# Two-block transformer kernel on one core: the second RG-LRU gate product emitted between the first SSD blocks, SSD's decayed rows taken straight from the transposed rows, dt rows on VectorE

## The chip, the cores and the metric

The kernel runs on one core of one Trainium2 chip. The metric is device time in microseconds, from the start of the one launch to its end. Six names for the units of the core are used below: PE (TensorE, the matmul engine; PEld is its weight load), DVE (VectorE), ACT (ScalarE), POOL (GpSimd), SP (SyncE, which here only issues DMAs) and the DMA engines. Each engine works through its own instruction list in the order written in the program, and waits where an operand is not there yet; so an instruction that waits holds up everything behind it on its engine.

## The reference, cut to what matters

Two transformer blocks on one sequence of 1024 rows of width 1024, in float32. The change lies in the mixer of the second block. Its input projection feeds three mixers side by side, whose outputs are joined and multiplied by `w_out`:

```
z, xbc, dt_raw, u_s5, x_rg, g_rg = split(h @ w_in)
# SSD: chunks of 128 rows, 8 heads of 64 channels, state of 128
xbc = silu(causal_dwconv(xbc));  xs, bm, cm = split(xbc)
dt  = softplus(dt_raw + dt_bias);  adt = -exp(a_log) * dt;  a_cs = cumsum(adt in the chunk)
xdt = xs * dt
y_diag = (cm bm^T * exp(a_cs_l - a_cs_s), lower triangle) xdt
states = bm^T (exp(a_cs_last - a_cs) * xdt)          # the decayed rows
state  = state * exp(a_cs_last) + states             # carried from chunk to chunk
y = (y_diag + exp(a_cs) * (cm state_before) + xs * d_skip) * silu(z);  y = rms_norm(y) * w
# RG-LRU: width 256
y_rg = linear_scan(a, b) * gelu(g_rg)
# then
y = concat(y_ssd, y_s5, y_rg) @ w_out;  h = layer_norm(ALPHA * h + y);  cross attention;  MLP
```

## The kernel before

Float32 products are made of three matmuls of reduced-precision halves: every operand is split into a high part (a cast on ACT, line 82) and a low part (a subtraction on DVE, line 83), and `mm3` issues high x high, high x low, low x high (lines 114, 115, 116). A tile of 128 rows by 1024 columns so costs one cast and one subtraction before PE can use it.

`build` is a list of stages written as generators. A scheduler orders the instructions of each engine ahead of the run, following the order in which the generators emit them and the times that it expects; the order is fixed once the kernel is built. Buffers come from pools with a fixed number of tiles for each tag (`BUFS`): a tile of tag S is reused after six others of that tag, so the emission order also decides which load waits for which reader.

The stages around the change, in the order of emission:

- `dt_proj` (line 1170) makes dt, adt and, in `s_exp`, three sets of exponentials; set 1 is the decay to the chunk's end.
- `xbc_proj` makes the eight feature tiles of xbc (matmuls, a convolution of three DVE operations at line 1216, a tanh on ACT at 1237, a product on DVE at 1238) and stores each to DRAM (`s_xbc`, line 1239). It is interleaved with `s5_mixer` and `rg_mixer`.
- `rg_mixer` ends with the gate: for each of the two halves (m = 0, 1) 48 matmuls, two ACT evictions for each 512 columns (1393, 1394), gelu (DVE 1325, 1326, ACT 1327, DVE 1328), the product with the scan (1396) and a store (`rg_od`, 1397). Both halves are emitted in one step.
- `wout_load` loads `w_out` as eight tiles of 128x1024 (512 KB each, line 668), splitting each.
- `ssd_block(i)`, i = 0 to 7, in three steps run as a pipeline by `pipe` (block i's first step is emitted ahead of block i-1's second). Step 1: load of the block from `s_xbc` (1254) and of z (1256), PE transposes (1260, 1264), products of the B and C rows (1266), ACT copies (1261, 1268), the masked C-B tile (DVE 1270), xdt and the decayed rows (both on POOL, 1274 and 1275), the decay matrix (ACT 446, PE 1283, ACT 1284) and its mask product for two groups of heads (DVE 1285). Step 2: PE 1291 (state), 1295 (states), 1298 (diagonal), the new state (DVE 1300, 1301), y (DVE 1303, 1304, 1306, 1307; the d_skip product on POOL at 1305). Step 3: square sum (ACT 1310), a reciprocal root as a chain of small DVE operations (135 to 141), scaling (DVE 1313), transposes (PE 1316), ACT 446, store to `s_od` (1319).
- `block2_out` is woven in behind: for each of 8 row tiles it loads the three mixers' outputs (686), splits them (82, 83), runs 48 matmuls against the `w_out` tiles, adds the residual (DVE 1067, with statistics at 155), normalises (165 to 170 on DVE, 171 on ACT) and transposes (PE 182, ACT 186).

The first row tile of `block2_out` can start its matmuls when SSD block 0 is through all three steps and the `w_out` tiles are split.

Of the kernel before, what the change touches and what calls it, by code (L numbers as in the profile page):

```python
# [10 lines left out]
ALU = mybir.AluOpType  # L11
# [6 lines left out]
NB = 8  # L18
# [1083 lines left out]
class Mix2(Mix1):  # L1102
# [67 lines left out]
    def dt_proj(self, T):  # L1170
        nc, I = self.nc, self.I
# [13 lines left out]
        dt = self.small([128, 64], tag="s_dt", bufs=1)  # L1185
# [12 lines left out]
            nc.tensor.matmul(out=ps[:, 64 * k:64 * k + 64], lhsT=l, rhs=adt, start=True, stop=True)  # L1198
        self.s_exp = self.small([128, 3, 64], tag="s_exp", bufs=1)
        nc.scalar.activation(out=self.s_exp.rearrange("p a b -> p (a b)"), in_=ps[:, 0:192], func=ACTF.Exp)  # L1200

    def z_tile(self, T, t):
        nc = self.nc
# [43 lines left out]
    def ssd_block(self, i):  # L1247
        nc = self.nc
        sl = slice(128 * i, 128 * i + 128)
        hs = slice(8 * i, 8 * i + 8)  # L1250
        bc64 = lambda a: a.unsqueeze(2).broadcast_to([128, 8, 64])
        v64 = lambda a: a.rearrange("p (h c) -> p h c", c=64)
# [4 lines left out]
        xt = self.page("H")  # L1257
# [7 lines left out]
        for g in range(2):  # L1265
# [5 lines left out]
                                in1=self.tri[:, 0].unsqueeze(1).broadcast_to([128, 2, 128]))  # L1271
        xx = self.page("S")
        xdt, xdec = v64(xx[:, 0:512]), v64(xx[:, 512:1024])
        nc.gpsimd.tensor_tensor(out=xdt, in0=v64(xt[:, 0:512]), in1=bc64(self.s_dt[:, hs]), op=ALU.mult)
        nc.gpsimd.tensor_tensor(out=xdec, in0=xdt, in1=bc64(self.s_exp[:, 1, hs]), op=ALU.mult)
        sg = self.ps("sc")
        Ts = []
        for g in range(2):
# [51 lines left out]
    def rg_mixer(self, T):  # L1330
        nc, I = self.nc, self.I
# [56 lines left out]
        for m, (xc, r, gx, t) in enumerate(ms):  # L1388
            x, q = self.page("X"), self.page("X")
            for h in range(2):  # L1390
                sl = slice(512 * h, 512 * h + 512)
                ps = self.feat_out(T, Wg, slice(128 * m, 128 * m + 128), h)
                nc.scalar.activation(out=x[:, sl], in_=ps, func=ACTF.Copy, scale=0.5)
                nc.scalar.activation(out=q[:, sl], in_=ps, func=ACTF.Square)
            self.gelu(x, q, q)
            nc.vector.tensor_tensor(out=t, in0=t, in1=q, op=ALU.mult)
            nc.sync.dma_start(out=self.rg_od[:, m, :], in_=t)

    def cmul(self, ore, oim, a, b, t, eng=None):

# [428 lines left out]
def build(tc, I, out):  # L1829
    from contextlib import ExitStack  # L1830
    with ExitStack() as ctx:
        n = Mix2(tc, ctx, I, out)
        n.modulation()
        n.kv_mem()
        def run(g):
            while True:
                try:
                    next(g)
                except StopIteration as e:
                    return e.value  # L1840

        def delay(g, k):
            for _ in range(k):
                yield
            yield from g

        norm, kv = n.first_norm(I["x"]), n.kv_proj()
        T, steps = None, [3, 0, 1, 0, 1]
        while T is None:
# [4 lines left out]
            T = next(norm)  # L1854
# [13 lines left out]
        T = run(n.block1_out())  # L1868
        T = n.block1_mlp(T)
        n.dt_proj(T)  # L1870
        xbc = n.xbc_proj(T)
        for g, side in ((n.s5_mixer(T), (3, 1)), (n.rg_mixer(T), (1, 3))):
            for _ in g:
                for _ in range(side[0] if side else 0):
                    next(xbc, None)
                side = side[1:]
        run(xbc)
        n.ssd_setup()
        n.wout = n.wout_load(I["w_out_2"])
        out = n.block2_out()  # L1880
        T = next(out)
        run(n.weave(n.pipe(n.ssd_block(i) for i in range(NB)), delay(out, 3)))
        T = run(n.attention(T))
        n.block2_mlp(T)

# [85 lines left out]
```

## Time and profile before

| | |
|---|---|
| time before, median of 3 runs | 2657.97 us (2657.94 to 2659.93) |
| the profiled execution's own time | 2657.86 us |
| its span in the trace | 2655.9 us |
| PE busy | 2541.6 us, 96% of the span |
| DVE busy | 1879.1 us, 71% |
| ACT busy | 1172.0 us, 44% |
| POOL busy | 239.3 us, 9% |
| mean granted PE clock | 0.979 of full speed |

PE is busy for 96% of the span, so time is lost or won only where PE stands still or runs at the lower clock. The shares are averages over stages with different limits: in the first SSD blocks, at about 1590 to 1635 us, DVE is nearly full and PE waits.

### The profile page before, as it was taken

The numbers are of one execution on the slowest core, as the hardware profiler recorded it, in microseconds if no ns is written. First come the engines' busy times: TensorE is split into PE (matmuls) and PEld (weight loads), VectorE is DVE, ScalarE is ACT, GpSimd is POOL, SyncE is SP. The second block draws the span as 40 slices with busy tenths as digits, with TensorE's granted clock in tenths as the row PEclk, the third lists the DMA queues.
The fourth block names the chain that finished last, engine by engine and source line by source line (L and its number), as shares of the span: only waits on it lengthen the run. The fifth ranks groups of instructions, "written<-read, shape, count | busy, mean of one in ns | idle before, by whom it ended". The sixth has DMA issues, their size and how long they took to land. (4 is left out here: it accounts for less than half of the span.)

```text
span 2655.9 us, 33016 instructions
## 1 busy us (share of the span) xinstructions
PE 2541.6 (96%) x12086; PEld 2065.0 (78%) x12086; DVE 1879.1 (71%) x3205; ACT 1172.0 (44%) x1866; POOL 239.3 (9%) x222
## 2 busy tenths in 40 slices
PE   7899999889999999999999998999998999999997
PEld 6586777677888888888877776778876888888886
DVE  4858666678897777646865567785568777767786
ACT  3622233344654444433643474552237454444342
POOL 4121135540000000000000003100000000000000
PEclk8899999999999999999999999999998999999999
DMA  9772433464266569866632243361102755799783
GB/s 334 253 256 100 146 100 99 140 168 149 78 230 222 195 231 328 305 192 229 199 149 64 82 143 115 116 222 56 40 32 88 256 191 210 245 341 337 263 284 106
DMA packets 255130, 484.36 MB, mean 182 GB/s; under 512 B 21604, under 2 KB 110964, under 8 KB 254968
## 3 DMA queue, kind: packets, MB, share of 16 engines
q1 hardware_dynamic: 247768, 470.59, 52.2%
q10 hardware_dynamic: 7200, 11.67, 1.2%
q8 instruction: 95, 1.56, 0.3%
q14 instruction: 67, 0.55, 0.1%
HBM read 338.80 MB, written 143.38 MB: 182 GB/s over the span
## 5 line engine op out<-in xcount | busy, mean ns | idle before, releaser
L114 PE MATMUL ps<-U,W 128*128 128x512 f32 (+1 forms) x1080 | 427.3, 396 | 10.4 <-ACT ev L776 5.1
L115 PE MATMUL ps<-U,W 128*128 128x512 f32 (+1 forms) x1080 | 425.6, 394 | 1.5 <-DVE U L341 1.5
L114 PE MATMUL ps<-W,H 128*128 128x512 f32 x1088 | 424.4, 390 | 0.4 <-DVE X L1069 0.3
L116 PE MATMUL ps<-U,W 128*128 128x512 f32 (+1 forms) x1080 | 423.5, 392 | 0.8 <-DVE W L83 0.8
L83 DVE TENSOR_TENSOR W<-S,W 128x1024 fp32r<-128x1024 f32 (+1 forms) x272 | 333.1, 1228 | 128.5 <-ACT W L82 127.5
L115 PE MATMUL ps<-W,H 128*128 128x512 f32 x1088 | 423.9, 390 | 0.0
L116 PE MATMUL ps<-W,H 128*128 128x512 f32 x1088 | 423.9, 390 | 0.0
L82 ACT CAST W<-S 128x1024 fp32r<-128x1024 f32 x288 | 298.6, 1043 | 242.2 <-PE ps L115 161.1
L82 ACT CAST H<-S 128x1024 fp32r<-128x1024 f32 x130 | 136.6, 1050 | 287.4 <-PE ps L115 200.7
L83 DVE TENSOR_TENSOR H<-S,H 128x1024 fp32r<-128x1024 f32 x130 | 158.6, 1220 | 146.0 <-ACT H L82 141.2
L114 PEld LDWEIGHTS ps<-U,W 128*128 128x128 f32 (+1 forms) x1080 | 201.2, 186 | 60.9 <-ACT ev L776 5.4
L115 PEld LDWEIGHTS ps<-U,W 128*128 128x128 f32 (+1 forms) x1080 | 201.2, 186 | 49.5 <-DVE U L341 4.6
L114 PEld LDWEIGHTS ps<-W,H 128*128 128x128 f32 x1088 | 204.3, 188 | 43.4 <-DVE X L1069 1.2
L116 PEld LDWEIGHTS ps<-U,W 128*128 128x128 f32 (+1 forms) x1080 | 201.2, 186 | 46.8 <-DVE W L83 1.9
L116 PEld LDWEIGHTS ps<-W,H 128*128 128x128 f32 x1088 | 204.3, 188 | 41.9
L115 PEld LDWEIGHTS ps<-W,H 128*128 128x128 f32 x1088 | 204.3, 188 | 41.7
L116 PE MATMUL ps<-W,U 128*128 128x512 f32 x352 | 139.8, 397 | 5.5 <-DVE U L83 5.5
L114 PE MATMUL ps<-W,U 128*128 128x512 f32 x352 | 141.8, 403 | 2.6 <-DVE X L274 2.0
L115 PE MATMUL ps<-W,U 128*128 128x512 f32 x352 | 140.3, 398 | 0.0
L776 ACT ACTIVATE ev<-ev 128x512 f32<-128x512 f32 x104 | 65.5, 630 | 152.4 <-DVE ev L874 122.5
L116 PEld LDWEIGHTS ps<-W,U 128*128 128x128 f32 x352 | 67.0, 190 | 20.7 <-DVE U L83 6.8
L777 ACT ACTIVATE X<-ev 128x512 f32<-128x512 f32 x128 | 81.0, 634 | 3.5
(529 smaller groups left out, 4505.1 us busy)
## 6 DMA issues: line engine op xcount, KB each, us to landing
S<-mlp_h SPq DMA_DIRECT2D x112, 512.0 KB, 5.1
S<-in_w_ff SPq DMA_DIRECT2D x96, 512.0 KB, 5.1
mlp_h<-X SPq DMA_DIRECT2D x96, 512.0 KB, 4.2
S<-in_mlp_w SPq DMA_DIRECT2D x96, 512.0 KB, 4.9
mlp_w<-S SPq DMA_DIRECT2D x96, 256.0 KB, 2.5
S<-mlp_w SPq DMA_DIRECT2D x48, 512.0 KB, 4.8
S<-in_w_in SPq DMA_DIRECT2D x46, 512.0 KB, 5.3
X<-in_w_ada SPq DMA_DIRECT2D x32, 512.0 KB, 6.8
```

What stands on the lines that cost most here:

```text
L82: self.nc.scalar.copy(out=hi, in_=src)
L83: (lo_eng or self.nc.vector).tensor_tensor(out=lo, in0=src, in1=hi.bitcast(F32), op=ALU.subtract)
L114: mm(out=ps, lhsT=lh, rhs=rh, start=start and k == 0, stop=False)
L115: mm(out=ps, lhsT=lh, rhs=rl, start=False, stop=False)
L116: mm(out=ps, lhsT=ll, rhs=rh, start=False, stop=stop and k == n - 1)
L776: nc.scalar.activation(out=r, in_=x, func=ACTF.Relu)
L777: nc.scalar.activation(out=out, in_=r, func=ACTF.Square)
```

## The change

Four edits. In `dt_proj` the decay exponentials of all blocks are multiplied by dt once, in place (one new 128x64 product on DVE). In `ssd_block` the decayed rows are then made from the transposed rows and this product, no longer from xdt; xdt itself moves from POOL to DVE. `rg_mixer` yields after each half of the gate. `build` runs the first gate half, then emits the first step of SSD block 0, then the second gate half, then the first step of block 1 and the second of block 0, and only then `wout_load`; the weave with `block2_out` starts after two steps less, which leaves it where it was in terms of SSD steps.

```diff
--- before.py
+++ after.py
@@ -1198,6 +1198,7 @@
             nc.tensor.matmul(out=ps[:, 64 * k:64 * k + 64], lhsT=l, rhs=adt, start=True, stop=True)
         self.s_exp = self.small([128, 3, 64], tag="s_exp", bufs=1)
         nc.scalar.activation(out=self.s_exp.rearrange("p a b -> p (a b)"), in_=ps[:, 0:192], func=ACTF.Exp)
+        nc.vector.tensor_tensor(out=self.s_exp[:, 1], in0=self.s_exp[:, 1], in1=dt, op=ALU.mult)
 
     def z_tile(self, T, t):
         nc = self.nc
@@ -1271,8 +1272,8 @@
                                 in1=self.tri[:, 0].unsqueeze(1).broadcast_to([128, 2, 128]))
         xx = self.page("S")
         xdt, xdec = v64(xx[:, 0:512]), v64(xx[:, 512:1024])
-        nc.gpsimd.tensor_tensor(out=xdt, in0=v64(xt[:, 0:512]), in1=bc64(self.s_dt[:, hs]), op=ALU.mult)
-        nc.gpsimd.tensor_tensor(out=xdec, in0=xdt, in1=bc64(self.s_exp[:, 1, hs]), op=ALU.mult)
+        nc.vector.tensor_tensor(out=xdt, in0=v64(xt[:, 0:512]), in1=bc64(self.s_dt[:, hs]), op=ALU.mult)
+        nc.gpsimd.tensor_tensor(out=xdec, in0=v64(xt[:, 0:512]), in1=bc64(self.s_exp[:, 1, hs]), op=ALU.mult)
         sg = self.ps("sc")
         Ts = []
         for g in range(2):
@@ -1395,6 +1396,7 @@
             self.gelu(x, q, q)
             nc.vector.tensor_tensor(out=t, in0=t, in1=q, op=ALU.mult)
             nc.sync.dma_start(out=self.rg_od[:, m, :], in_=t)
+            yield
 
     def cmul(self, ore, oim, a, b, t, eng=None):
 
@@ -1869,17 +1871,25 @@
         T = n.block1_mlp(T)
         n.dt_proj(T)
         xbc = n.xbc_proj(T)
-        for g, side in ((n.s5_mixer(T), (3, 1)), (n.rg_mixer(T), (1, 3))):
-            for _ in g:
-                for _ in range(side[0] if side else 0):
-                    next(xbc, None)
-                side = side[1:]
+        side = [3, 1]
+        for _ in n.s5_mixer(T):
+            for _ in range(side.pop(0) if side else 0):
+                next(xbc, None)
+        rg = n.rg_mixer(T)
+        for k in (1, 3, 0, 0):
+            next(rg)
+            for _ in range(k):
+                next(xbc, None)
         run(xbc)
         n.ssd_setup()
+        ssd = n.pipe(n.ssd_block(i) for i in range(NB))
+        next(ssd)
+        run(rg)
+        next(ssd)
         n.wout = n.wout_load(I["w_out_2"])
         out = n.block2_out()
         T = next(out)
-        run(n.weave(n.pipe(n.ssd_block(i) for i in range(NB)), delay(out, 3)))
+        run(n.weave(ssd, delay(out, 1)))
         T = run(n.attention(T))
         n.block2_mlp(T)
```

How this moves the instructions. Two lines are inserted ahead of `build`: the lines named above as 1201 to 1397 are one higher in the changed kernel (1260 is 1261 there, 1285 is 1286), those behind 1397 two higher.

The list of PE before, at the end of the second gate half (`ps_12863` is its last product) and the start of SSD block 0 (`H_12952`):

```order
L114 MATMUL ps_12863<-U_6173,W_12521 128x512
L115 MATMUL ps_12863<-U_6174,W_12521 128x512
L116 MATMUL ps_12863<-U_6173,W_12522 128x512
L1260 MATMUL ps_12957<-ident,H_12952 128x128 x4
L1264 MATMUL ps_12963<-ident,H_12952 128x128 x2
L1266 MATMUL ps_12963<-H_12952 128x128 x2
L1283 MATMUL ps_12973<-half_12982,tri 128x512
L1283 MATMUL ps_13011<-half_13020,tri 128x512
L1291 MATMUL ps_13028<-half_12896,H_12952 128x256 x2
L1283 MATMUL ps_13070<-half_13071,tri 128x512
L1260 MATMUL ps_12995<-ident,H_12990 128x128 x4
```

And now, where the first product of the second gate half (`ps_12878`) is under way; `H_12838` is SSD block 0:

```order
L116 MATMUL ps_12878<-U_6171,W_12517 128x512
L114 MATMUL ps_12878<-U_6171,W_12516 128x512
L115 MATMUL ps_12878<-U_6172,W_12516 128x512
L1261 MATMUL ps_12843<-ident,H_12838 128x128 x4
L1265 MATMUL ps_12849<-ident,H_12838 128x128 x2
L1267 MATMUL ps_12849<-H_12838 128x128 x2
L116 MATMUL ps_12878<-U_6171,W_12517 128x512
L114 MATMUL ps_12878<-U_6171,W_12522 128x512
L115 MATMUL ps_12878<-U_6172,W_12522 128x512
L116 MATMUL ps_12878<-U_6171,W_12523 128x512
L114 MATMUL ps_12878<-U_6171,W_12522 128x512
```

Block 0's transposes stood behind the whole second gate half; they now stand after 11 of its 48 matmuls, and the other 37 stand behind them.

The list of DVE before, from the first gate half's last product (1396) on; the rows of line 83 split `w_out` tiles:

```order
L1396 TENSOR_TENSOR H_12528<-H_12528,X_12773 128x1024
L83 TENSOR_TENSOR X_12913<-S_12911,X_12912 128x1024
L83 TENSOR_TENSOR X_12919<-S_12917,X_12918 128x1024
L83 TENSOR_TENSOR W_12925<-S_12923,W_12924 128x1024
L83 TENSOR_TENSOR X_12937<-S_12935,X_12936 128x1024
L83 TENSOR_TENSOR W_12931<-S_12929,W_12930 128x1024
L1325 TENSOR_SCALAR X_12835<-X_12835 128x1024
L1270 TENSOR_TENSOR H_12956<-ps_12963,tri 128x256
L1326 TENSOR_TENSOR X_12835<-X_12835,X_12834 128x1024
L1285 TENSOR_TENSOR half_12974<-half_12974,H_12956 128x512
```

And now, from the second gate half's gelu (1327) on; `H_12942` is SSD block 1, line 1275 is xdt, the last row splits the first `w_out` tile:

```order
L1326 TENSOR_SCALAR X_12877<-X_12877 128x1024
L1275 TENSOR_TENSOR S_12956<-H_12942,s_dt_11569 128x512
L1327 TENSOR_TENSOR X_12877<-X_12877,X_12876 128x1024
L1271 TENSOR_TENSOR H_12942<-ps_12949,tri 128x256
L1301 TENSOR_TENSOR half_12835<-half_12835,s_exp_11603 128x512
L1286 TENSOR_TENSOR half_12960<-half_12960,H_12942 128x512
L1329 SCALAR_TENSOR_TENSOR X_12877<-X_12877,X_12876 128x1024
L1286 TENSOR_TENSOR half_12968<-half_12968,H_12942 128x512
L1397 TENSOR_TENSOR H_12546<-H_12546,X_12877 128x1024
L1302 TENSOR_TENSOR half_12835<-ps_12979,half_12835 128x512
L1304 TENSOR_TENSOR H_12838<-ps_12976,s_exp_11603 128x512
L83 TENSOR_TENSOR W_12999<-S_12997,W_12998 128x1024
```

The `w_out` splits, of which seven stood ahead of block 0's C-B tile and one behind the gate, now all stand behind the gate and block 0's state update, the first at the place shown and the other seven among blocks 0, 1 and 2.

The list of DVE before in the stretch in which row tile 2 of `block2_out` is split (`U_13216`) beside SSD block 5 (`half_13478`, `half_13486`) and step 2 of block 4 (`H_13273`):

```order
L1285 TENSOR_TENSOR half_13486<-half_13486,H_13460 128x512
L1301 TENSOR_TENSOR half_12896<-ps_13497,half_12896 128x512
L1303 TENSOR_TENSOR H_13273<-ps_13494,s_exp_11603 128x512
L170 TENSOR_SCALAR sm_13542<-sm_13540,sm_13544 128x1
L1304 TENSOR_TENSOR H_13273<-ps_13494,H_13273 128x512
L83 TENSOR_TENSOR U_13216<-S_13579,U_13215 128x8x128
L1306 TENSOR_TENSOR H_13273<-H_13273,H_13277 128x512
L1307 TENSOR_TENSOR H_13273<-H_13273,ev_13275 128x512
```

And the same stretch now, up to the split (`U_13217`):

```order
L1286 TENSOR_TENSOR half_13487<-half_13487,H_13461 128x512
L1302 TENSOR_TENSOR half_12835<-ps_13498,half_12835 128x512
L1304 TENSOR_TENSOR H_13274<-ps_13495,s_exp_11603 128x512
L139 TENSOR_SCALAR rs_13546<-rs_13546 128x1
L1305 TENSOR_TENSOR H_13274<-ps_13495,H_13274 128x512
L140 TENSOR_SCALAR rs_13546<-rs_13546 128x1
L1307 TENSOR_TENSOR H_13274<-H_13274,H_13278 128x512
L141 TENSOR_SCALAR sm_13545<-rs_13546,sm_13545 128x1
L1308 TENSOR_TENSOR H_13274<-H_13274,ev_13276 128x512
L170 TENSOR_SCALAR sm_13543<-sm_13541,sm_13545 128x1
L83 TENSOR_TENSOR U_13217<-S_13580,U_13216 128x8x128
```

Two products of block 4's y (1306 and 1307, here 1307 and 1308) stood behind the split and now stand ahead of it, and so does, some rows further up, block 5's xdt (1275 here). Of the same kind is a shift at row tile 0: block 4's C-B tile, its two mask products and block 3's state sum, which stood ahead of row tile 0's residual sums, now stand between those sums and the statistics' end (165).

## Rows read from the trace of the kernel before

**Rows 1.** Stretches: busy time of PE, PEld, DVE, ACT, POOL, then clock, DMA.

```profile
1571.40:1590.40 19.00, 18.69 (x82) 14.69 (x81) 14.97 (x14) 10.99 (x16) 0.00 (x0) 1.00 0.82 271
1590.40:1634.60 44.20, 33.95 (x176) 24.72 (x174) 40.37 (x69) 23.84 (x58) 18.08 (x13) 0.92 0.36 109
```

**Rows 2.** PE timeline: start, duration, line, tiles, idle before it and releaser.

```profile
1589.69 0.39 PE L114 MATMUL ps<-U,W 128*128 128x512 f32 x1
...
1590.15 0.39 PE L116 MATMUL ps<-U,W 128*128 128x512 f32 x1
...
1604.24 1.11 PE L1260 MATMUL ps<-ident,H 128*128 128x128 f32 x4 [0.38 <-DVE H L1270]
...
1633.30 1.10 PE L1295 MATMUL ps<-S,H 128*128 128x256 f32 x4 [0.23 <-ACT H L1261]
1634.24 0.60 PE L1316 MATMUL ps<-ident,H 128*128 128x128 f32 x4
...
1637.13 0.50 PE L116 MATMUL ps<-W,U 128*128 128x512 f32 x1 [1.37 <-DVE U L83]
...
1669.69 0.50 PE L116 MATMUL ps<-W,U 128*128 128x512 f32 x1 [2.21 <-DVE U L83]
...
1690.70 0.50 PE L116 MATMUL ps<-W,U 128*128 128x512 f32 x1 [1.94 <-DVE U L83]
...
1712.36 0.47 PE L116 MATMUL ps<-W,H 128*128 128x512 f32 x1
```

**Rows 3.** DVE timeline from the convolution's end to the first row tile.

```profile
1573.71 3.91 DVE L1216 SCALAR_TENSOR_TENSOR bc<-S,hw,bc 128x1023 f32<-128x1023 f32 x3
1578.81 1.23 DVE L1238 SCALAR_TENSOR_TENSOR bc<-S,bc 128x1024 f32<-128x1024 f32 x1 [1.19 <-ACT S L1237]
...
1583.44 1.22 DVE L1328 SCALAR_TENSOR_TENSOR X<-X,X 128x1024 f32<-128x1024 f32 x1 [1.19 <-ACT X L1327]
...
1593.81 1.73 DVE L1326 TENSOR_TENSOR X<-X,X 128x1024 f32<-128x1024 f32 x1
1595.46 2.97 DVE L1285 TENSOR_TENSOR half<-half,H 128x512 f32<-128x512 f32 x2
...
1635.02 2.06 DVE L83 TENSOR_TENSOR U<-S,U 128x1024 fp32r<-128x1024 f32 x1
```

**Rows 4.** POOL by line, 1571 to 1830 us: count, busy, mean ns, idle before.

```profile
L1305 POOL TENSOR_TENSOR H<-H,srow 128x512 f32<-128x512 f32 x8 | 12.1, 1510 | 0.0
L1275 POOL TENSOR_TENSOR S<-S,s_exp 128x512 f32<-128x512 f32 x8 | 10.4, 1306 | 0.6
L1274 POOL TENSOR_TENSOR S<-H,s_dt 128x512 f32<-128x512 f32 x8 | 9.9, 1233 | 253.4 <-ACT H L1261 253.4
```

**Rows 5.** SP timeline (the last xbc store, the first block's load).

```profile
1580.06 0.34 SPq L1239 DMA_DIRECT2D s_xbc<-bc  x1
...
1583.37 0.56 SPq L1254 DMA_DIRECT2D H<-s_xbc  x1
```

**Rows 6.** Line 1254, the loads of SSD blocks: time from issue to landing.

```profile
DMA to landing us min/median/max: 4.0/4.7/7.5
```

**Rows 7.** Line 668, the `w_out` loads: time from issue to landing.

```profile
DMA to landing us min/median/max: 3.3/4.7/8.1
```

**Rows 8.** DVE timeline beside row tiles 2 and 4.

```profile
1662.58 1.33 DVE L1285 TENSOR_TENSOR half<-half,H 128x512 f32<-128x512 f32 x1
1663.84 1.53 DVE L1300 TENSOR_TENSOR half<-half,s_exp 128x512 f32<-128x512 f32 x1
...
1668.42 1.22 DVE L83 TENSOR_TENSOR U<-S,U 128x1024 fp32r<-128x1024 f32 x1
1669.56 0.68 DVE L1306 TENSOR_TENSOR H<-H,H 128x512 f32<-128x512 f32 x1
1670.27 0.69 DVE L1307 TENSOR_TENSOR H<-H,ev 128x512 f32<-128x512 f32 x1
...
1710.45 1.22 DVE L83 TENSOR_TENSOR H<-S,H 128x1024 fp32r<-128x1024 f32 x1
```

## Prediction, made before the changed kernel was run

> **What bounds the kernel now.** I read the page's shares first, then the stretches around the change, then in them the PE and DVE timelines, and POOL and SP where they feed these. PE is the bound of the whole, so I ask where PE stands still. From 1571 to 1590 us it runs the gate products and hardly waits (18.69 busy of 19.00); from 1590.4 to 1634.6, the first SSD blocks, it is busy for 33.95 of 44.20 us, at a mean clock of 0.92 [rows 1]. There 10.25 us are idle, and some of the busy time is slow: four transposes take 1.11 us at 1604.24 [rows 2]. In the same stretch DVE is busy for 40.37 of 44.20 us. The wait that ends it is PE's for the low half of row tile 0, at 1637.13, a DVE split of 2.06 us [rows 2, 3]. From there PE is full but for two waits of 2.21 and 1.94 us, both again for a DVE split (row tiles 2 and 3) [rows 2]. So around this change DVE's list sets PE's time: before the first row tile, and again in each later period.
>
> **The change part by part.** I work it out against the profiled execution's own 2657.86 us, 0.1 below the median, and speak of before's line numbers.
>
> *The place of block 0 (the first hole).* Now DVE runs two `w_out` splits between the last two tiles of xbc; they go, so the last convolution starts when the tile before is done, about 1571.6 instead of 1573.71. From that start to the end of the product took 1580.04 - 1573.71 = 6.33 us [rows 3], so the last store is issued at 1577.9. In the trace the first block's load follows that store by 1580.06 to 1583.37, 3.3 us [rows 5], so the load is issued at 1581.2; the shortest landing is 4.0 us, the median 4.7 [rows 6]. I take 4.0, since the `w_out` loads no longer run beside it: it lands at 1585.2. PE, which now need not wait for ACT's casts, starts the first gate half's second product at about 1572.9; matmuls follow each other by (1590.15 - 1589.69)/2 = 0.23 us [rows 2], so its 24 end at 1578.3, and the moved decay product (0.5) and 11 matmuls at 1581.4. Block 0's transposes stand next in PE's list. PE stands still for 3.8 us and with it the 37 gate matmuls queued behind. With 1.3 us for block 0's eight small products and 37 x 0.23 they end at 1595, where they ended at 1590.5 before.
>
> *DVE's holes.* Ahead of the first row tile DVE idled 4.0 us in the first stretch and 3.8 in the second [rows 1]. Now: 1.2 for ACT's tanh in the last xbc tile and 1.2 in gelu, both as now [rows 3]; 1.6 until the gate's first half is evicted (PE ends at 1578.3, and I estimate 1.2 for ACT's two operations); 3.0 from gelu's end (1583.8) until block 0's products are there (1586.8), since its C-B tile stands next; and 4.5 from block 0's mask products (about 1591.8) until the second gate half is evicted (1596.3), since gelu stands next. The `w_out` splits that filled this time now stand behind it. That is 11.5 us against 7.8, +3.7.
>
> *xdt on DVE.* Eight products of 128x512 of two SBUF inputs; one such takes 0.68 us alone [rows 8]. Four (blocks 0 to 3) lie ahead of the first row tile, +2.7. The one new product on dt is 64 columns wide, in the S5 stage ahead of all this, where DVE waits for PE; nothing.
>
> *POOL has eight operations less* of 1.23 us each [rows 4]. They slow DVE: in block 5 two products that take 0.68 alone took 1.33 and 1.53 [rows 8], and around 1595 the two mask products took 2.97 and gelu's product 1.73 instead of 1.22 [rows 3]. Block 5's 1.5 us over three POOL operations is 0.5 for each. Ahead of the first row tile 15 POOL operations become 8 (block 4's three now come later), so 7 x 0.5 = 3.5 us come back.
>
> The Trainium skill, page "SBUF — State Buffer", section "SBUF: two separate sides", says that a POOL operation and a DVE operation with two SBUF inputs take a shared pair of ports as an exclusive lock: the one that starts first keeps the other out for its whole length. The trace agrees where 1.33 is 0.68 and a wait of 0.65 [rows 8]. By that rule xdt on DVE and the decayed rows on POOL, now both released by the same ACT copy, meet in every block, and xdt may cost 0.68 + 1.23 us where the rows' 0.5 make it 1.2: for four blocks up to 2.8 us more in the sum below, which lies inside its bounds.
>
> *What moves behind the first row tile on DVE:* block 4's first mask product (0.68) and C-B tile (half as wide, an estimate of 0.4), -1.1. The `w_out` splits at last wait for loads: the last four are issued behind the second gate store (about 1604) and behind readers of blocks 0 and 1, and land 4.7 us later in the median [rows 7]; I estimate 0.4.
>
> Sum for the first row tile: 3.7 + 2.7 - 3.5 - 1.1 + 0.4 = **+2.2 us**. Bounds: with no relief from POOL +5.7; with each relief worth 0.85, the largest row, and the load's hole gone, -3.5.
>
> *PE work left over.* While PE waited for row tile 0 it did block 4's last product, block 3's state products and block 2's transposes. These now stand behind tile 0's 48 matmuls: 1633.30 to 1634.24, 0.9 [rows 2], 0.4 for the transposes and 0.2, **+1.5**. They also hide the later end of tile 0's statistics: block 4's C-B tile (0.4), two mask products and block 3's state sum (3 x 0.6) now stand ahead of it, 2.2 us, against 1.5 of that work and two matmuls that PE now has ahead of the transposes at 182. Nothing; at most 1.5.
>
> *Row tiles 2 and 3.* Ahead of the split now stand xdt (0.68) and y's last two products (0.6 each by the spacing of starts), 1.9; the reciprocal root's three small steps, which ran alone between 1665.3 and 1665.9, lie between the others, an estimate of -0.3. POOL's two operations instead of three: two products now collide with the one that is left and the d_skip product, so I take no relief. So the split at 1668.42 comes 1.5 us later and PE's waits of 2.21 and 1.94 grow by as much: **+3.0** for both. Bounds: 1.2 with a relief of 0.9 in each, 4.5 with full collisions.
>
> *Row tile 4.* Its split ends at 1711.67, its first use is at 1712.36 [rows 2, 8]: 0.7 us of slack under 1.5 us of delay, **+0.8** (0 to 1.5). Later tiles have no SSD step 1 beside them.
>
> Sum: 2.2 + 1.5 + 3.0 + 0.8 = 7.5 us, or 2665 us.
>
> **The rivals.**
>
> *Faster.* PE's chain through the first blocks, not DVE's list, sets the stretch: then taking block 0's first step out of it, one POOL operation of 1.23 us out of each block's way, and a PE kept denser (no 1.11 us transposes) count. Of PE's 10.25 idle us I let 8 come back, with all later delays hidden in port relief: 2650 us. For it: the slow rows and the waits on PE in the stretch. Against it: DVE is busy for 40.37 of 44.20 us. It decides at row tile 0's split: if that starts before 1629, this is it.
>
> *Nothing measurable.* The later delays are half as large, because each POOL operation left costs DVE less than two did, and the first row tile keeps its time, since block 0's load lands while PE is still at the 11 matmuls: about 2.5 us, 2660 us. For it: the relief is the least known term. Against it: the load cannot be issued before the last store has landed.
>
> *The `w_out` tiles come late.* The last four loads wait for tiles that blocks 0 and 1 release, and each landing of 8.1 instead of 4.7 us [rows 7] stops DVE's whole list with SSD's products in it. For it: the last four move 2 MB, 7.7 us at the 271 GB/s of the stretch [rows 1], and are issued within some 4 us. Against it: DVE needs the last of them only at about 1616. I price it at the difference of the rates, 4 us: 2669 us.
>
> **How the numbers follow.** The forecast, the sum with its bounds (2661 to 2668), 50%; late `w_out` tiles 14%; nothing measurable 23%; faster 13%. The predicted time is the sum, 2665 us. 0.2% is 5.3 us, about what a measurement here can tell from no change: 2652.7 to 2663.3. Slower: most of the forecast (42 of 50) and the late tiles, 56%. Same: the rest of the forecast and "nothing", with little of the faster case, 33%. Faster: 11%. The range, 2653 to 2673 us, takes in the late tiles with their own spread, the case of nothing and the edge of the faster one; the forecast's own range is 2661 to 2668.
>
> **What the profile after would show.** Right: PE waits 3 to 4 us for block 0's load inside the second gate half, whose end moves from 1590.5 to about 1595; DVE idles before block 0's C-B tile and again before the second gelu; row tile 0's low half is ready at about 1639 instead of 1637.1; the waits for the splits of row tiles 2 and 3 are near 3.5 us, and one of under 1 us appears at row tile 4. Wrong: no wait inside the gate half; row tile 0 before 1634 (then DVE's list was not the limit, or POOL's relief is larger than 0.5 for each operation); waits at row tiles 2 and 3 that do not grow (then the moved products were paid for by ports); a wait for `w_out` on ACT of more than 1 us (then the third rival).

## The result, and the profile after

The changed kernel takes 2674.27 us, median of 5 runs (2672.35 to 2675.79), against 2657.94 us (5 runs, 2656.12 to 2659.93): ratio 1.0061, interval 1.0046 to 1.0076, 16.3 us slower. The profiled execution has 2674.27 us and a span of 2672.2. The forecast was 2665, with 2673 as the top of its range: the direction was right, the size more than twice too small. After's lines are those of before plus one up to 1397 (1302 is the new state, 1292 its product on PE).

The PE timeline after, with the places of [rows 2]; start, duration, line, tiles, idle before and releaser.

```profile
1586.56 0.66 PE L1261 MATMUL ps<-ident,H 128*128 128x128 f32 x4 [2.90 <-DMA H<-s_xbc]
...
1588.63 0.63 PE L114 MATMUL ps<-U,W 128*128 128x512 f32 x1
...
1599.74 1.03 PE L1292 MATMUL ps<-half,H 128*128 128x256 f32 x4
...
1625.39 2.05 PE L1292 MATMUL ps<-half,H 128*128 128x256 f32 x4 [10.87 <-DVE half L1302]
1627.23 3.52 PE L1299 MATMUL ps<-S,half 128*128 128x64 f32 x16
...
1645.28 0.50 PE L116 MATMUL ps<-W,U 128*128 128x512 f32 x1
...
1669.15 0.60 PE L1261 MATMUL ps<-ident,H 128*128 128x128 f32 x4
...
1680.38 0.80 PE L116 MATMUL ps<-W,U 128*128 128x512 f32 x1 [3.33 <-DVE sm L1312]
1680.98 0.63 PE L114 MATMUL ps<-W,U 128*128 128x512 f32 x1
1681.40 0.63 PE L115 MATMUL ps<-W,U 128*128 128x512 f32 x1
1681.83 1.91 PE L182 MATMUL ps<-ident,H 128*128 128x128 f32 x8
...
1705.55 0.50 PE L116 MATMUL ps<-W,U 128*128 128x512 f32 x1 [3.34 <-DVE sm L1312]
1706.35 1.61 PE L182 MATMUL ps<-ident,H 128*128 128x128 f32 x8
...
1729.61 0.50 PE L116 MATMUL ps<-W,H 128*128 128x512 f32 x1 [0.74 <-DVE H L83]
```

Five waits of these rows are new or longer. The one for block 0's load (2.90; forecast as 3 to 4), those of row tiles 2 and 3 (3.33 and 3.34, where [rows 2] has 2.21 and 1.94) and the 0.74 at row tile 4 were forecast; DVE's row before the latter is the split of line 83 (1679.12 to 1680.34), though the view names a small operation behind it. The 10.87 us for block 1's state sum were not. And behind these waits stand rows at the lower clock: 2.05 us for a product that takes 1.03 at 1599.74, matmuls of 0.63 where they take 0.39, and 1.91 us for eight transposes that took 1.03 in the kernel before:

```profile
1670.26 1.03 PE L182 MATMUL ps<-ident,H 128*128 128x128 f32 x8
```

The DVE timeline after, for [rows 3]:

```profile
1588.85 0.42 DVE L1271 TENSOR_TENSOR H<-ps,tri 128x256 f32<-128x256 f32 x1 [3.07 <-ACT H L1269]
...
1599.09 0.69 DVE L1326 TENSOR_SCALAR X<-X 128x1024 f32<-128x1024 f32 x1 [6.03 <-ACT X L1395]
...
1607.22 0.68 DVE L1302 TENSOR_TENSOR half<-ps,half 128x512 f32<-128x512 f32 x1
...
1608.42 1.21 DVE L83 TENSOR_TENSOR W<-S,W 128x1024 fp32r<-128x1024 f32 x1
...
1621.63 1.21 DVE L83 TENSOR_TENSOR X<-S,X 128x1024 fp32r<-128x1024 f32 x1
...
1624.57 0.68 DVE L1302 TENSOR_TENSOR half<-ps,half 128x512 f32<-128x512 f32 x1
...
1630.79 0.69 DVE L1304 TENSOR_TENSOR H<-ps,s_exp 128x512 f32<-128x512 f32 x1 [1.17 <-PE ps L1299]
...
1635.10 0.69 DVE L1275 TENSOR_TENSOR S<-H,s_dt 128x512 f32<-128x512 f32 x1 [1.38 <-ACT H L1262]
...
1636.65 0.42 DVE L1271 TENSOR_TENSOR H<-ps,tri 128x256 f32<-128x256 f32 x1 [0.85 <-ACT H L1269]
...
1644.00 1.22 DVE L83 TENSOR_TENSOR U<-S,U 128x1024 fp32r<-128x1024 f32 x1
```

The eight `w_out` splits (1608.42 to 1621.63) stand between block 0's state sum and block 1's, for which PE waits. Ahead of them DVE idles for 3.07 and 6.03 us; from 1599 to 1629 it hardly does; then it waits for the slow PE.

From the start of the last convolution to the split of row tile 0, first before, then after (length; busy time and count of PE, PEld, DVE, ACT, POOL; clock, DMA share, GB/s):

```profile
1573.71:1635.02 61.31, 50.88 (x248) 38.31 (x247) 53.45 (x81) 32.67 (x71) 18.48 (x14) 0.94 0.50 157
```

```profile
1573.07:1644.00 70.93, 52.48 (x240) 40.37 (x238) 52.45 (x82) 33.96 (x70) 11.23 (x8) 0.86 0.50 159
```

DVE worked 1.0 us less, and idled 18.48 us (70.93 - 52.45) instead of 7.86 (61.31 - 53.45).

**Where the kernels part.** Single executions already differ by some us at the RG-LRU's second scan on DVE, most of it in the first 600 us; up to there the lists of PE, DVE, ACT and POOL of before and after agree but for the 64-column product (of the DMA issues, three `w_out` loads come later). So I count from the start of that scan, at 1565.66 us before and 1567.27 after, to a row, and subtract before's value: row tile 0's first low product, for instance, (1645.28 - 1567.27) - (1637.13 - 1565.66) = +6.5 us. The end is that of the span. The table has these differences in us, from one profile of each kernel, with median and ratio (interval) against the kernel before on the same chip.

| kernel | median, us | ratio | scan | row tile 0 | block 5 | block 6 | block 7 | end |
|---|---|---|---|---|---|---|---|---|
| after | 2674.27 | 1.0061 (1.0046-1.0076) | +1.6 | +6.5 | +8.0 | +11.8 | +14.9 | +14.7 |
| after, once more | 2672.84 | 1.0050 (1.0037-1.0063) | +3.3 | +6.8 | +8.2 | +12.1 | +15.1 | +14.2 |
| order only | 2671.53 | 1.0049 (1.0037-1.0062) | +6.0 | +9.8 | +9.7 | +9.5 | +9.4 | +8.5 |
| engines only | 2670.97 | 1.0050 (1.0036-1.0065) | +2.8 | +3.5 | +3.5 | +4.6 | +7.6 | +6.6 |
| late `w_out` only | 2673.89 | 1.0057 (1.0044-1.0070) | +5.3 | +11.3 | +11.3 | +12.6 | +12.6 | +11.5 |
| half of `w_out` first | 2672.60 | 1.0056 (1.0044-1.0068) | +5.3 | +4.2 | +6.8 | +9.5 | +12.6 | +15.3 |
| first wait filled | 2673.60 | 1.0059 (1.0044-1.0074) | +3.5 | +4.3 | +6.6 | +7.7 | +10.7 | +9.9 |
| row tiles filled | 2670.11 | 1.0041 (1.0029-1.0053) | +2.2 | +4.7 | +6.1 | +7.8 | +9.8 | +10.0 |
| after, splits on POOL | 2672.70 | 1.0054 (1.0040-1.0068) | +4.9 | +4.9 | +6.3 | +8.4 | +11.0 | +12.8 |
| before, splits on POOL | 2657.74 | 0.9998 (0.9989-1.0007) | +3.4 | -0.4 | -0.4 | -0.7 | -0.8 | -1.6 |
| unchained on POOL | 2656.60 | 0.9992 (0.9982-1.0002) | +1.0 | -0.6 | -0.6 | -0.7 | -0.8 | -2.1 |
| before, rows first | 2710.93 | 1.0187 (1.0171-1.0204) | | | | | | |
| after, rows first | 2717.31 | 1.0217 (1.0203-1.0231) | | | | | | |

(Block 5, 6 and 7: the start of their transposes. The kernel before ran for 2658.53, 2656.88 and 2659.79 us in median beside the three sets of experiments.)

### The profile page after: what moved, and what is told of

It is laid out like the page before. It is cut to its first block, busy times and chain, and to the rows that moved or that the text cites. A ratio compares the mean times of both kernels' runs of the same rounds, so it can differ in the third digit from the quotient of the medians.

```text
span 2672.2 us, 33023 instructions
## 1 busy us (share of the span) xinstructions
PE 2545.0 (95%) x12086; PEld 2069.4 (77%) x12086; DVE 1884.5 (71%) x3214; ACT 1173.7 (44%) x1866; POOL 229.7 (9%) x214
## 4 chain that ended last, share of the span: by engine, by line
PE 74%; DVE 12%; ACT 5%; DMA 4%; issue 3%; POOL 2%; SPq 0%; DVEq 0%; ACTq 0%; POOLq 0%
PE ps L116 23%; PE ps L114 23%; PE ps L115 23%; DMA H<-g_qkb 1%; POOL X L531 1%; PE ps L182 1%; DVE W L83 1%; DVE half L552 1%; DMA H<-r_qk 1%; ACT half L186 1%; DVE st L155 1%; PE ps L544 1%; DMA S<-in_xa_wk 1%; DVE U L341 0%; DVE bc L1217 0%
```

## The experiments

Theory A: the changed order alone makes row tile 0 late, since the `w_out` splits no longer fill DVE's gaps, and xdt on DVE makes only the splits of row tiles 2 and 3 late, where the lower clock multiplies the loss. Theory B: xdt makes the first blocks late too. Theory C: no part of the periods' growth is clock.

**The two halves apart.** Order only: the changed kernel with both products on POOL again.

```diff
-        nc.vector.tensor_tensor(out=self.s_exp[:, 1], in0=self.s_exp[:, 1], in1=dt, op=ALU.mult)
...
-        nc.vector.tensor_tensor(out=xdt, in0=v64(xt[:, 0:512]), in1=bc64(self.s_dt[:, hs]), op=ALU.mult)
-        nc.gpsimd.tensor_tensor(out=xdec, in0=v64(xt[:, 0:512]), in1=bc64(self.s_exp[:, 1, hs]), op=ALU.mult)
+        nc.gpsimd.tensor_tensor(out=xdt, in0=v64(xt[:, 0:512]), in1=bc64(self.s_dt[:, hs]), op=ALU.mult)
+        nc.gpsimd.tensor_tensor(out=xdec, in0=xdt, in1=bc64(self.s_exp[:, 1, hs]), op=ALU.mult)
```

> The changed order of emission, with both SSD products on POOL as in the kernel before. Theory A (the order alone makes the first row tile late: the w_out splits and the second gelu stand on DVE between block 0's and block 1's state sums, PE waits about 11 us for the second of them and then runs at the lower clock; row tiles 2 and 3 are the business of xdt): PE's wait for block 1's state sum is 8 to 11 us, the low half of row tile 0 is first used 6 to 9 us later than before, PE's waits at row tiles 2 and 3 stay at 2.2 and 1.9 us; 2664 to 2670 us. Theory B (xdt on DVE is what makes the first blocks late, the order costs only the two holes that were forecast): row tile 0 2 to 4 us later than before, 2660 to 2663 us.

Engines only: the kernel before with these lines the other way round and its own `build`.

> The order of emission of before, with xdt on DVE and the decayed rows straight from the transposed rows. Theory A: row tile 0 within 2 us of before, no wait of PE over 4 us in the first blocks; PE's waits at row tiles 2 and 3 grow to 3 us or more and rows at the lower clock follow them, so that each period grows by 3 to 4 us; 2663 to 2667 us. Theory B: row tile 0 4 to 6 us later than before, and the row tiles' loss on top: 2668 to 2672 us.

With the order only, row tile 0 came 9.8 us later and nothing was lost behind it: the waits at row tiles 2 and 3 were 1.93 us each. A's place is right, its size somewhat short (6 to 9, and 2664 to 2670 us against 2671.53), and the wait for block 1's state sum was only 4.51 us, not 8 to 11, so that long wait is not needed for the loss:

```profile
1629.61 2.05 PE L1291 MATMUL ps<-half,H 128*128 128x256 f32 x4 [4.51 <-DVE half L1301]
```

With the engines only, row tile 0 came 3.5 us later, between A's 2 and B's 4, the periods from block 5 to 6 and 6 to 7 grew by 1.2 and 3.0, and the median, 2670.97, lies in B's range and not in A's. So in the order of before xdt on DVE does make the first blocks later; on top of the changed order it does not (row tile 0 at +6.5 with it, +9.8 without). PE in the two periods:

```profile
1677.07 0.50 PE L116 MATMUL ps<-W,U 128*128 128x512 f32 x1 [3.33 <-DVE sm L1312]
...
1677.88 1.04 PE L182 MATMUL ps<-ident,H 128*128 128x128 f32 x8
...
1699.50 0.80 PE L116 MATMUL ps<-W,U 128*128 128x512 f32 x1 [3.34 <-DVE sm L1312]
...
1700.95 1.91 PE L182 MATMUL ps<-ident,H 128*128 128x128 f32 x8
```

Two equal waits: behind the first PE runs on at full clock and the period lasts 22.4 us, behind the second at the lower one and it lasts 24.0. At the end of the span the halves add up (8.5 + 6.6 = 15.1, against 14.7), but that is luck: at row tile 0 they make 9.8 + 3.5 = 13.3 against 6.5, at block 6 9.5 + 4.6 = 14.1 against 11.8, and the medians 13.0 + 12.4 = 25.4 us over the kernel before, against 16.3. The halves are not independent.

**Which part of the order.** Late `w_out` only: the order of before, with the loads and splits emitted behind two SSD steps.

```diff
-        n.wout = n.wout_load(I["w_out_2"])
+        ssd = n.pipe(n.ssd_block(i) for i in range(NB))
+        next(ssd)
+        next(ssd)
+        n.wout = n.wout_load(I["w_out_2"])
         out = n.block2_out()
         T = next(out)
-        run(n.weave(n.pipe(n.ssd_block(i) for i in range(NB)), delay(out, 3)))
+        run(n.weave(ssd, delay(out, 1)))
```

> The kernel before with one part of the order changed: w_out is loaded and split behind the first steps of blocks 0 and 1, while the gate halves stay together and both SSD products stay on POOL. If the late w_out splits are what the changed order costs (theory A): DVE idles where they stood (before blocks 0's products), row tile 0 is 6 to 9 us later from the second scan on, about as in the kernel with the changed order alone (9.7 us later); 2664 to 2668 us. If the other part, block 0's first step between the gate halves with PE's wait for its load and DVE's wait for the second gelu, is what costs: row tile 0 is less than 4 us later, 2658 to 2662 us.

Row tile 0 came 11.3 us later, no less than with the whole order (9.8): the late `w_out` alone is enough for the loss. Place as theory A has it, size above it (6 to 9; 2673.89 us against 2664 to 2668). Whether block 0's step between the gate halves gave the other 1.5 us back isn't shown, since the lower clock held for longer here (0.75 in the stretch below, 0.86 with the whole order). DVE idles where the splits stood, and does them later, beside POOL:

```profile
1595.99 0.69 DVE L1325 TENSOR_SCALAR X<-X 128x1024 f32<-128x1024 f32 x1 [5.25 <-ACT X L1394]
...
1621.33 4.04 DVE L83 TENSOR_TENSOR W<-S,W 128x1024 fp32r<-128x1024 f32 x2
```

From the last convolution to row tile 0's split, the windows of the same kernel:

```profile
1576.75:1652.46 75.71, 61.69 (x252) 46.96 (x251) 56.95 (x82) 34.89 (x72) 20.47 (x14) 0.75 0.51 163
```

18.76 us idle, about as in the changed kernel (18.48), against 7.86 before, but made up otherwise: 7.3 us (2.02 and 5.25) are waits for the gate's two evictions, where the kernel before has 0.26, none, and 1.26 ahead of a split, and 6.5 us (1.74, 2.17 and 2.61) come behind 1637, where DVE waits for a PE whose mean clock is 0.59 from 1634 on. So late splits hold up PE, and PE, slower behind its waits, holds up DVE in turn.

**Half of `w_out` first.** In the changed kernel four tiles go ahead of the second gate half. All eight need every buffer of tags W and X, which that half still uses, so this wasn't tried.

```diff
         next(ssd)
+        n.wout = n.wout_load(I["w_out_2"], None, (0, 4))
         run(rg)
         next(ssd)
-        n.wout = n.wout_load(I["w_out_2"])
+        n.wout_load(I["w_out_2"], None, (2, 6), n.wout)
```

> The changed kernel with four of the eight w_out tiles loaded and split ahead of the second gate half, where DVE idles for 6.0 us; the other four stay where they are. Theory A (DVE's list between the two state sums is what holds up PE): PE's wait for block 1's state sum falls from 10.9 us to 5 to 7 us, row tile 0 is 3 to 5 us earlier than in the changed kernel, 2669 to 2671 us. Theory B (xdt on DVE): row tile 0 moves by less than 1.5 us, 2673 to 2675 us.

PE's longest wait for a state sum fell to 2.75 us, with 2.65 at another; row tile 0 came 2.4 us earlier than in the first profile after, and 1.2 of it were lost again by block 5. The time is between both theories: the edit didn't settle it.

**Does the lower clock cost?** First wait filled: 16 more products on PE in the wait for block 1's state sum.

```diff
+        if i == 2:
+            self.xt2 = xt[:, 0:512]
...
+        if i == 3:
+            fill = self.ps()
+            for _ in range(16):
+                nc.tensor.matmul(out=fill, lhsT=self.ones, rhs=self.xt2, start=True, stop=True)
         yield
         yy = self.ps("sc")
```

> The changed kernel with 16 more float32 products of 128x512 on PE ahead of block 2's state product (their result is not used), some 13 us of PE work in the wait of 10.9 us and the smaller ones before it. Theory A1 (the lower clock behind that wait is a good part of the first row tile's delay): the rows behind it run at the full clock (the next state product in 1.03 us for four, not 2.05), and, from the second scan on DVE on, row tile 0's low half is used 2 to 4 us earlier than in the changed kernel; 2670 to 2672 us. Theory A2 (DVE's list alone sets the first row tile, PE's clock is hidden behind it): the rows are faster, row tile 0 moves by less than 1 us; 2673 to 2675 us, or later where the added products themselves delay something.

The wait is full and the rows behind it fast (a product shows as two instructions; 14 of the 32 found room earlier):

```profile
1618.48 7.89 PE L1293 MATMUL ps<-H,ones 128*128 128x512 f32 x18
1626.20 1.03 PE L1298 MATMUL ps<-half,H 128*128 128x256 f32 x4
```

Row tile 0 is 2.2 us earlier than in the first profile after, as A1 has it; but in this execution the gate matmuls behind the first wait ran at full clock too. Two executions of kernels with the changed kernel's lists up to row tile 0 had that without filling, and stand at +4.7 and +4.9, so filling itself gained about half a us, and the median, 2673.60, lies in A2's range. From the last convolution to row tile 0's split, first one of these two (row tiles filled, below), then this one:

```profile
1573.62:1642.69 69.07, 50.88 (x241) 39.23 (x240) 52.61 (x82) 33.96 (x70) 11.23 (x8) 0.88 0.51 164
1574.99:1643.53 68.54, 61.88 (x285) 43.30 (x285) 54.79 (x84) 34.83 (x72) 13.60 (x10) 1.00 0.54 172
```

DVE's idle time fell from 16.5 to 13.8 us and its busy time rose from 52.6 to 54.8. Part of that rise is order: block 4's xdt (1.53 us) and C-B tile (0.41) and block 3's state sum (0.67), behind the split in the changed kernel, stand ahead of it here. So the run doesn't separate the two theories: with PE at full clock throughout (1.00) row tile 0 is still 4.3 us late, but up to 2.6 of that may be these three products. What it does show is how DVE's idle time divides: of the 10.6 us more than before in the first profile after, 5.9 (13.75 against 7.86) are left at full clock.

Row tiles filled: 13 more matmuls ahead of the second half of row tiles 2 and 3.

```diff
                 ps = self.ps()
+                if n == 1 and i in (2, 3) and len(srcs) == 3:
+                    for _ in range(13):
+                        nc.tensor.matmul(out=ps, lhsT=M[0][:, 0, :], rhs=W[n][0][0], start=True, stop=True)
```

> The changed kernel with 13 more matmuls of 128x512 ahead of the second half of row tiles 2 and 3 (their result is overwritten), about 3.0 us of PE work in waits of 3.3 us. Theory A (the lower clock behind a wait of 3.3 us costs more than the growth of the wait): the matmuls behind the wait run at 0.23 us from start to start, the periods shrink from 25.2 and 24.1 us to about 22.4 each, 2669 to 2671 us. Theory C (the growth of the periods is DVE's lateness alone, and the slow rows are covered by other waits): the time stays within 1 us of the changed kernel's, 2673 to 2675 us.

The two periods, from block 5's transposes to 6's and to 7's (windows, columns as above), before, after and filled:

```profile
1659.58:1680.86 21.28, 19.07 (x99) 15.20 (x98) 15.60 (x33) 12.24 (x30) 3.54 (x3) 1.00 0.30 83
1680.86:1701.89 21.03, 19.09 (x99) 15.20 (x98) 15.34 (x33) 12.37 (x30) 3.53 (x3) 1.00 0.40 128
```

```profile
1669.15:1694.31 25.16, 21.83 (x100) 17.36 (x99) 15.44 (x34) 12.80 (x32) 2.09 (x2) 0.86 0.36 116
1694.31:1718.37 24.06, 20.72 (x99) 16.54 (x98) 15.45 (x34) 12.35 (x30) 2.09 (x2) 0.93 0.33 99
```

```profile
1667.83:1690.84 23.01, 22.18 (x112) 17.57 (x111) 15.45 (x34) 12.81 (x32) 2.09 (x2) 1.00 0.40 126
1690.84:1713.84 23.00, 22.18 (x113) 17.57 (x112) 15.44 (x34) 12.36 (x30) 2.09 (x2) 1.00 0.35 104
```

More work on PE, at clock 1.00 instead of 0.86 and 0.93, and each period is shorter, by 2.2 and 1.1 us (A had 22.4 for each, 0.6 less than came). The median, 2670.11, lies in A's range, 4.2 below the first runs of the changed kernel and 2.7 below the second; the intervals of the ratios overlap, so the periods are the firmer sign. C falls.

**The splits on POOL,** in the kernel before and in the changed one:

```diff
-            self.split(st, M[0], M[1])
+            self.split(st, M[0], M[1], nc.gpsimd if i in (2, 3) and len(srcs) == 3 else None)
```

> The kernel before with the low halves of row tiles 2 and 3 made on POOL instead of DVE, where they wait for no other product. Theory (DVE's list, not the data, makes these splits late): a split of 2.4 to 3 us starts on POOL when the cast is done, at the place of the DVE products ahead of it, PE's waits of 2.2 and 1.9 us fall below 1 us each; 2654 to 2656 us. Rival (POOL's split takes longer than it saves, or slows DVE's products and the statistics behind it): waits unchanged or longer, 2657 to 2661 us.

> The same edit on the changed kernel. Theory: PE's waits of 3.33 and 3.34 us fall below 1.5 us, no rows at the lower clock behind them, periods of about 21.5 us instead of 25.2 and 24.1; 2667 to 2669 us. Rival as for the kernel before: periods stay above 24 us, 2673 to 2676 us.

Before, the wait for the split fell to 0.17 us, and one of 1.5 us came up for the normalised row at line 182, so that nothing measurable was won. After, the same with 2.61 us, and the lower clock again behind it:

```profile
1684.66 1.97 PE L182 MATMUL ps<-ident,H 128*128 128x128 f32 x8 [2.61 <-ACT H L171]
```

Both expectations of a gain in time failed, though the changed kernel's periods went down to 23.4 and 23.6 us. The rival's half on DVE came true: while POOL ran its split, the mask product beside it on DVE, ahead of the normalisation's last step (170), took 2.25 and 2.46 us before and 2.71 and 2.43 after, where it takes 0.68 otherwise. Here row tile 2, before and after:

```profile
1668.91 2.25 DVE L1285 TENSOR_TENSOR half<-half,H 128x512 f32<-128x512 f32 x1
```

```profile
1676.56 2.71 DVE L1286 TENSOR_TENSOR half<-half,H 128x512 f32<-128x512 f32 x1
```

That is 1.6 to 2.0 us more, beside new waits of 1.5 and 2.6 us for the normalised row.

**Unchained on POOL.** The kernel before with the product on dt and the decayed rows from the transposed rows, everything on POOL.

```diff
-        nc.gpsimd.tensor_tensor(out=xdec, in0=xdt, in1=bc64(self.s_exp[:, 1, hs]), op=ALU.mult)
+        nc.gpsimd.tensor_tensor(out=xdec, in0=v64(xt[:, 0:512]), in1=bc64(self.s_exp[:, 1, hs]), op=ALU.mult)
```

> The kernel before with the decayed rows straight from the transposed rows and both products still on POOL, so that POOL's second product no longer needs the first one's result and DVE gets no xdt. Theory (xdt on DVE is what costs at the row tiles; that the two products no longer hang together is worth nothing, since POOL works them one behind the other anyway): from the second scan on DVE on, row tile 0 within 1 us of before, PE's waits at row tiles 2 and 3 at 2.2 and 1.9 us, 2656 to 2660 us. Rival (the direct product changes the lateness of the state products): more than 2 us off at row tile 0.

As expected: row tile 0 within 0.6 us, no measurable change of the time. So what the engines-only kernel costs (+6.6 at the end of the span), it costs through xdt on DVE.

**Row tiles ahead of the SSD step,** in the kernel before (and, with `delay(out, 1)` and `ssd`, in the changed one):

```diff
-        run(n.weave(n.pipe(n.ssd_block(i) for i in range(NB)), delay(out, 3)))
+        run(n.weave(delay(out, 3), n.pipe(n.ssd_block(i) for i in range(NB))))
```

> The kernel before with each row tile of the output projection emitted ahead of the SSD step of the same round instead of behind it, so that its split and its normalisation stand ahead of that step's products on DVE. Theory (DVE's list order, not DVE's load, makes PE wait in these periods): PE's waits of 2.2 and 1.9 us for the splits of row tiles 2 and 3 fall below 0.5 us, each period shrinks by 1 to 2 us, 2653 to 2656 us. Rival (the SSD products that now stand behind become late instead: PE waits for a mask product or a state sum, or the normalisation's transposes wait): periods as before or longer, 2657 to 2662 us.

> The same edit on the changed kernel. Theory: the waits of 3.33 and 3.34 us fall below 1 us, no rows at the lower clock behind them, the two periods shrink from 25.2 and 24.1 us to 20.5 to 22; the first row tile keeps its delay; 2665 to 2669 us. Rival: the periods stay above 23.5 us, 2672 to 2676 us.

Both failed by far, +51 and +58 us over the kernel before. Waits for splits are no longer among PE's long ones, but PE now waits for the normalised row, here in the kernel before with this edit:

```profile
1699.85 1.97 PE L182 MATMUL ps<-ident,H 128*128 128x128 f32 x8 [5.04 <-ACT H L171]
```

The SSD matmuls no longer stand between a row tile's last matmuls and its transposes, where they had covered the normalisation. The edit moves too much to tell anything of the list's order alone. No version in the table is faster than the kernel before, clear of the noise.

**The changed kernel once more:**

> The changed kernel once more, for a second profile. If the rows at the lower clock behind PE's waits of 2.9 to 3.4 us are a matter of the single execution, this profile has them behind some of the three waits and not behind others, and a period without them lasts 22.4 us; if they are a fixed consequence of the wait, all three waits have them and the periods are 24 to 25 us again. 2672 to 2676 us by both.

The same waits, all three with the lower clock behind them, and every place behind the scan within 0.5 us of the first profile. By the expectation that spoke for a fixed consequence of the wait; the equal waits with the engines only, and with the first wait filled, say otherwise (last section).

## Why the prediction was wrong

From the scan on, the first profile after has +6.5 for row tile 0, +1.4 behind it, +6.9 in the two periods and -0.2 from there to the end; the 1.6 us that stood ahead of the scan are not the change's as far as the lists go, and make up the 16.3.

- *First row tile, +2.2 us: mis-sized, +6.5.* The failed step is the term for DVE's holes, 11.5 against 7.8 and 0.4 for `w_out`: measured 18.48 against 7.86, +10.6 instead of +4.1. The five holes that the prediction listed were there, 13.5 us in all: 3.07 before the C-B tile (3.0 forecast), 2.02 before the first gelu (1.6), 6.03 before the second (4.5), and the two of 1.2. What they have beyond 11.5 is clock, which was not priced: without slow rows behind the wait for block 0's load they are 11.4 us (row tiles filled) and 11.7 us (first wait filled); the hole before the second gelu is 4.78 us in the latter, where block 0's transposes to block 1's take 9.6 instead of 11.2 us, and row tile 0 stands at +4.7 and +4.9 in the two executions with the changed kernel's lists and no slow rows there. Another 4.0 us lie behind 1629 (1.17, 1.38, 0.85 and 0.58; the view puts the last down to a load, but the product reads rows of PE that end just then, at 1641.11), where DVE waits for a PE that comes late, at the lower clock behind the wait of 10.87 us; with the first wait filled 1.2 of them are left (0.29, 0.15, 0.79). The prediction stopped counting at the second gelu and took PE at full clock. The other items: the convolution starts 2.2 us earlier from the scan on, since the two `w_out` splits ahead of it (2.3 us) now lie behind it, DVE's work from there is 1.0 less, the split takes 1.22 instead of 2.06 us; 10.6 - 2.2 - 1.0 - 0.8 = 6.6. The experiments show what makes the holes cost: `w_out` late alone, without block 0's early step, costs 11.3.
- *xdt +2.7, POOL's relief -3.5, moved products -1.1: together -4.1 instead of -1.9.* Counted from start to start on DVE, the four xdt take 3.4 us, what moved behind the split is worth some 2.0, and the other products and the split give back some 5.5. This hides a part of what the holes cost. The relief hangs on the order: with the engines only, DVE's work up to the split rises from 53.45 to 56.12 us, by five xdt (3.9) less one mask product, and next to nothing comes back; with the late `w_out` it falls from 54.94 (order only) to 52.45, though four xdt come on top and only some 1.9 move behind the split, so about 4 come back. Why wasn't tested.
- *PE work behind row tile 0, +1.5:* +1.4.
- *Row tiles 2 and 3, +1.5 each: the wait right, its price wrong.* The waits grew by 1.1 and 1.4 us, the periods by 3.9 and 3.0. The step that failed is pricing a wait by its own length: what is missing, 4.4 us, are rows at the lower clock. Filling the waits took 3.2 us off, and in the engines-only kernel the period without slow rows grew by 1.2 us for a wait that grew by 1.1.
- *Row tile 4, +0.8:* a wait of 0.74 us; at the end of the span it is made up for.
- *The rivals.* "Faster" was wrong by its own sign: row tile 0's split started at 1644, far behind 1629. "Nothing measurable" fell with row tile 0's +6.5. Late `w_out` loads were not seen: no cast on ACT waited for one, and DVE waited 0.6 us for one cast. The port rule was weighed as up to 2.8 us: of the first four xdt three took 0.69 us or less and one 1.53, but the other four took 1.53, 1.40, 1.40 and 1.40, each while POOL ran the decayed rows, so it met in five blocks of eight.
- *The bounds.* The lower bound of the first term adds up to -3.25, not -3.5. The bounds of the four terms together give about 2657 to 2673 us, not 2661 to 2668; the measured 2674.27 lies outside both.

## What to carry to other kernels

Before moving work on an engine that runs its list in order, ask what filled its gaps where the work stood: here eight splits (9.2 us of DVE work) that looked movable were the filling of 9 us of gaps, and behind the gaps their work came on top. Price a longer wait of PE with the matmuls behind it at half rate as well, not only with its own length (1.6 to 2.7 us here, where it happened). And follow each stall to what is late next: taking the splits of two row tiles off DVE brought up the wait for their normalisation.

## What was not expected of the hardware

The length of a wait alone does not tell whether the lower clock follows. At the wait for block 0's load it followed 2.77 us (order only), 2.89 (half of `w_out` first) and 2.90 us (both profiles after), and did not follow 2.62 (row tiles filled), 2.83 (first wait filled) and 2.96 us (after, splits on POOL); at the row tiles 3.33 us had it in the changed kernel and not, once each, with the engines only and with the first wait filled; 1.93 us had it with late `w_out` only, and did not with the order only. In one and the same execution a row tile's period was 1.6 us longer with it than without: 24.0 and 22.4 us (engines only), 24.1 and 22.4 (first wait filled), 22.6 and 21.0 (late `w_out` only). The mean granted clock of the four us behind, in the first profile after and in that with the splits on POOL:

```profile
1586.50:1590.50 4.00, 3.94 (x16) 3.46 (x17) 1.65 (x3) 0.96 (x2) 1.05 (x1) 0.59 0.24 58
```

```profile
1589.80:1593.80 4.00, 3.91 (x22) 3.42 (x23) 2.15 (x3) 0.96 (x2) 1.04 (x1) 1.00 0.21 54
```

The clock is near its lower level (1.2 GHz) in one and at the full 2.4 GHz in the other. The Trainium skill, page "TensorE: Matmul & The Clock Gate", section "Part 1: The HAM clock gate (the "warmup" mystery)", says that an idle PE falls back to half of its clock and that activity releases it; the trace agrees behind 10.87 us (2.05 us for 1.03).
